# Cross entropy of 256 x 32000 logits on one core: two rows per partition, fourteen loads of shrinking size, one activation table set, and a store without a transpose

## The chip, the core and the metric

The kernel runs on one core of a Trainium2 chip. A core has a matrix engine (TensorE, in the profile PE), a vector engine (VectorE, DVE), an engine for functions such as exp and log (ScalarE, ACT), a general one (GpSimd, POOL), and SyncE (SP), which here only issues transfers. Transfers between the chip's memory and the core's own memory (SBUF, 128 partitions) are moved by 16 DMA engines, whichever engine issued them. Each engine works through its own list in order and waits on semaphores. The metric is the device time of one execution in microseconds, the median of several runs.

## What is computed

The inputs are 256 rows of 32000 float32 logits and one label per row. The result is, for each row, the negative log probability of the label:

```python
log_probs = logits - np.max(logits, axis=-1, keepdims=True)
log_probs = log_probs - np.log(np.sum(np.exp(log_probs), axis=-1, keepdims=True))
return np.array([-log_probs[i, labels[i]] for i in range(batch)]).astype(np.float32)
```

Both kernels leave out the maximum and compute log(sum(exp(x)) * exp(-g)), where g is the row's logit at its label. The logits are 32.77 MB, and each is read once.

## The kernel before

A tile holds one row of logits per partition, so there are two groups of rows, r = 0 (rows 0 to 127) and r = 1 (rows 128 to 255). The columns are cut into eight chunks: six of 4400, one of 3201, one of 2399. The loop goes over the chunks, and in each over the two groups; a step loads 128 x chunk (L120, issued by SP) and takes the exponential in place, with the sum over the row as a second output (L125, on ACT). In the trace such an exponential is two instructions: ACTIVATE, and ACTIVATION_READ_ACCUMULATOR, which writes the sum. Seven buffers of 4400 columns let SP run ahead of ACT; a load into a buffer that was used before waits for the exponential that read it.

Beside this, per group: the labels are loaded by GpSimd's queue (L75, 128 pieces of 8 B, since a label is 64 bits), GpSimd adds the row's offset (L78, L84) and issues an indirect transfer (L87) that gathers g, one float per partition; ACT makes eg = exp(-g) (L94). After the seventh chunk DVE adds up the seven partial sums (L135) and multiplies by eg (L138); this is the bias. When the last sum s_last is there, ACT makes log(s_last * eg + bias) (L143). The order on ACT at the end is chosen by the scheduler of the framework: last exponential of the first group, its logarithm, last exponential of the second group, its logarithm. Exponential and logarithm are taken from two different activation tables, and the compiler puts an ACT_TABLE_LOAD where the function changes.

At the very end the two columns of results (128 partitions x 2) are transposed on TensorE (L152) with an identity matrix made at the start by GpSimd, copied out of its result memory by DVE (L154), and stored by SP as two pieces of 512 B (L157).

Loads share eight semaphores in turn (DMAHW0 to DMAHW7 in the listings below). A load whose semaphore is still in use by an earlier transfer waits until that one has landed.

Of the kernel before, what the change touches and what calls it, by code (L numbers as in the profile page):

```python
# [3 lines left out]

# [5 lines left out]

P = 128

_PLAN = os.environ.get("CE_CHUNKS", "")


def _chunk_plan(C):
    if _PLAN:
        sizes = [int(x) for x in _PLAN.split(",")]
        assert sum(sizes) == C, (sizes, sum(sizes), C)
        return sizes  # L20
    sizes = []
    rem = C
    while rem > 4400 * 2:
        sizes.append(4400)
        rem -= 4400
    if rem > 0:
        a = (rem * 4 + 7) // 7
        a = min(a, rem)
        b = rem - a
        sizes.append(a)  # L30
        if b > 0:
            sizes.append(b)
    assert sum(sizes) == C
    return sizes


@with_exitstack
def kernel(
    ctx: ExitStack,
    tc: tile.TileContext,  # L40
    logits: bass.AP,
    labels: bass.AP,
    out: bass.AP,
):
    nc = tc.nc

    B, C = logits.shape
    n_row_tiles = (B + P - 1) // P
    assert B % P == 0, "only multiples of 128 supported for now"

    sizes = _chunk_plan(C)
    n_chunks = len(sizes)
    F_MAX = max(sizes)

    n_bufs = min(12, max(3, (128 * 1024) // (F_MAX * 4)))
    chunks = ctx.enter_context(tc.tile_pool(name="chunks", bufs=n_bufs))
    small = ctx.enter_context(tc.tile_pool(name="small", bufs=2 * n_row_tiles))
    out_pool = ctx.enter_context(tc.tile_pool(name="outp", bufs=1))

    singles = ctx.enter_context(tc.tile_pool(name="singles", bufs=1))  # L60
    psum_pool = ctx.enter_context(tc.tile_pool(name="psum", bufs=1, space=bass.MemoryType.PSUM))
    id_tile = singles.tile([P, P], mybir.dt.float32)
    make_identity(nc, id_tile[:, :])

    gathered = []
    lbl_t32 = dataclasses.replace(
        labels.tensor,
        shape=[labels.tensor.shape[0] * 2],
        dtype=mybir.dt.int32,
    )  # L70
    for r in range(n_row_tiles):
        r0 = r * P
        lbl = small.tile([P, 2], mybir.dt.int32)
        lbl_dram = bass.AP(tensor=lbl_t32, offset=r0 * 2, ap=[[2, P], [1, 2]])
        nc.gpsimd.dma_start(out=lbl[:, :], in_=lbl_dram)  # L75

        idx = small.tile([P, 1], mybir.dt.int32)
        nc.gpsimd.iota(  # L78
            out=idx[:, :],
            pattern=[[0, 1]],  # L80
            base=r0 * C,
            channel_multiplier=C,
        )
        nc.gpsimd.tensor_add(out=idx[:, :], in0=idx[:, :], in1=lbl[:, 0:1])  # L84

        g = small.tile([P, 1], mybir.dt.float32)
        nc.gpsimd.indirect_dma_start(  # L87
            out=g[:, :],
            out_offset=None,
            in_=logits[:, :],  # L90
            in_offset=bass.IndirectOffsetOnAxis(ap=idx[:, 0:1], axis=1),
        )
        eg = small.tile([P, 1], mybir.dt.float32)
        nc.scalar.activation(  # L94
            out=eg[:, :], in_=g[:, :], func=mybir.ActivationFunctionType.Exp,
            scale=-1.0,
        )
        gathered.append(eg)

    n_bulk = n_chunks - 1  # L100
    partials = [
        small.tile([P, max(1, n_bulk)], mybir.dt.float32, name=f"partial{r}")
        for r in range(n_row_tiles)
    ]
    s_last = [
        small.tile([P, 1], mybir.dt.float32, name=f"s_last{r}")
        for r in range(n_row_tiles)
    ]
    bias_r = [
        small.tile([P, 1], mybir.dt.float32, name=f"bias{r}")  # L110
        for r in range(n_row_tiles)
    ]
    res_all = out_pool.tile([P, n_row_tiles], mybir.dt.float32)

    c0 = 0
    for c, fc in enumerate(sizes):
        for r in range(n_row_tiles):
            r0 = r * P
            x = chunks.tile([P, F_MAX], mybir.dt.float32)
            nc.sync.dma_start(out=x[:, :fc], in_=logits[r0:r0 + P, c0:c0 + fc])  # L120
            if c < n_bulk:
                acc = partials[r][:, c:c + 1]
            else:
                acc = s_last[r][:, :]
            nc.scalar.activation(  # L125
                out=x[:, :fc],
                in_=x[:, :fc],
                func=mybir.ActivationFunctionType.Exp,
                accum_out=acc,
            )  # L130
        c0 += fc
        if c == n_bulk - 1:
            for r in range(n_row_tiles):
                ps = small.tile([P, 1], mybir.dt.float32, name=f"psum{r}")
                nc.vector.reduce_sum(  # L135
                    out=ps[:, :], in_=partials[r][:, :], axis=mybir.AxisListType.X
                )
                nc.vector.tensor_mul(  # L138
                    out=bias_r[r][:, :], in0=ps[:, :], in1=gathered[r][:, :]
                )  # L140

    for r in range(n_row_tiles):
        nc.scalar.activation(  # L143
            out=res_all[:, r:r + 1],
            in_=s_last[r][:, :],
            func=mybir.ActivationFunctionType.Ln,
            scale=gathered[r][:, :],
            bias=bias_r[r][:, :],
        )

    res_t_psum = psum_pool.tile([n_row_tiles, P], mybir.dt.float32, space=bass.MemoryType.PSUM)
    nc.tensor.transpose(out=res_t_psum[:, :], in_=res_all[:, :], identity=id_tile[:, :])  # L152
    res_t = out_pool.tile([n_row_tiles, P], mybir.dt.float32)
    nc.vector.tensor_copy(out=res_t[:, :], in_=res_t_psum[:, :])  # L154

    out_view = out.rearrange("(r p) -> r p", p=P)
    nc.sync.dma_start(out=out_view, in_=res_t[:, :])  # L157


# [1 line left out]
_INS = ['logits', 'labels']  # L161
_OUTS = [((256,), 'float32')]


# [23 lines left out]
```

## Time and profile before

| what | value |
|---|---|
| time, median of 3 runs | 91.57 us (91.46 to 91.59) |
| span of the profiled execution, first to last instruction | 89.6 us |
| median less that span | 1.97 us |
| ACT busy | 63.9 us, 71% of the span |
| POOL busy | 4.5 us |
| DVE and PE busy | 0.9 us and 0.4 us |
| memory read | 32.77 MB, mean 366 GB/s over the span |

The profile gives no time of the profiled execution other than its span; what lies around the span is taken as the difference to the median. A row of the timeline or the chain has start and duration in us, then the engine, the line (L120 is line 120 of the kernel), the operation and "output <- input". SPq stands for SP's list of DMA issues. "[6.86 <-DMA x]" means that the engine stood idle for 6.86 us before and that a load of x ended it. In the rows of groups the numbers are total busy us and mean ns of one. In the rows of windows come the stretch, the busy time of each engine, the clock of TensorE, the DMA share and GB/s.

### The profile page before, as it was taken

How to read it: one execution, taken by the hardware profiler on the slowest of the kernel's cores; microseconds unless marked ns; L12 is line 12 of the kernel's file. 1: busy time of each engine (PE TensorE's matmuls, PEld its weight loads, DVE VectorE, ACT ScalarE, POOL GpSimd, SP SyncE). 2: the span in 40 equal slices, each digit the busy share in tenths (PEclk: the TensorE clock that was granted, in tenths of full speed). 3: DMA queues.
4: the chain of work that ended last, by engine and by line, in shares of the span. 5: the costliest groups of instructions: out<-in, count | busy, mean ns of one | idle time of the engine just before them, and what ended most of it. 6: DMA issues, size and time to landing. Idle time of an engine off the chain costs nothing.

```text
span 89.6 us, 147 instructions
## 1 busy us (share of the span) xinstructions
PE 0.4 (0%) x1; PEld 0.1 (0%) x1; DVE 0.9 (1%) x5; ACT 63.9 (71%) x40; POOL 4.5 (5%) x14
## 2 busy tenths in 40 slices
PE   0000000000000000000000000000000000000010
PEld 0000000000000000000000000000000000000000
DVE  0000000000000000000000000000000010100010
ACT  5000970199999894949769494976949978999950
POOL 5300630000000000000000000000000000000000
DMA  5799999999999999999999999999999999920000
GB/s 118 306 433 393 432 424 417 440 432 416 440 416 448 416 456 416 424 432 424 448 409 424 448 424 440 424 440 416 424 424 423 417 419 428 433 103 0 0 0 0
DMA packets 2436, 32.77 MB, mean 366 GB/s; under 512 B 386, under 2 KB 388, under 8 KB 388
## 3 DMA queue, kind: packets, MB, share of 16 engines
q1 hardware_dynamic: 2308, 32.77, 86.5%
q0 software_dynamic: 128, 0.00, 0.1%
HBM read 32.77 MB, written 0.00 MB: 366 GB/s over the span
## 4 chain that ended last, share of the span: by engine, by line
DMA 74%; ACT 15%; issue 3%; SPq 3%; ACTq 0%; PE 0%; DVE 0%
DMA x<-in_logits_dram 74%; ACT x L125 10%; SPq L120 3%; ACT L143 3%; ACT L125 1%; ACTq L183 0%; PE res_t_psum L152 0%; DVE res_t L154 0%; ACT res_all L143 0%; ACTq L125 0%
## 5 line engine op out<-in xcount | busy, mean ns | idle before, releaser
L125 ACT ACTIVATE x<-x 128x4400 f32<-128x4400 f32 (+2 forms) x16 | 56.5, 3533 | 17.1 <-DMA x<-in_logits_dram 17.0
L94 ACT ACTIVATE eg<-g 128x1 f32<-128x1 f32 x2 | 0.4, 202 | 4.7 <-DMA g<-in_logits_dram,idx 4.7
L125 ACT ACT_TABLE_LOAD x2 | 2.6, 1283 | 0.8 <-PEq L172 0.7
L125 ACT ACTIVATION_READ_ACCUMULATOR x<-x 128x1 f32 x16 | 3.0, 187 | 0.0
L143 ACT ACT_TABLE_LOAD x2 | 2.6, 1283 | 0.0
L87 POOL DMA_INDIRECT g<-in_logits_dram,idx x2 | 2.0, 999 | 0.8 <-DMA lbl<-in_labels_dram 0.5
L75 POOL DMA_DIRECT2D lbl<-in_labels_dram x2 | 1.3, 655 | 0.4 <-issue 0.4
L135 DVE TENSOR_REDUCE psum<-partial 128x1 f32<-128x7 f32 x2 | 0.3, 160 | 76.9 <-ACT x L125 76.9
L143 ACT ACTIVATE res_all<-s_last,bias,eg 128x1 f32<-128x1 f32 x2 | 0.8, 386 | 0.0
L152 PE MATMUL res_t_psum<-id_tile,res_all 128*2 128x128 f32 x1 | 0.4, 371 | 86.6 <-ACT res_all L143 86.6
L84 POOL TENSOR_TENSOR idx<-idx,lbl 128x1 int32<-128x1 int32 x2 | 0.4, 192 | 5.8 <-DMA lbl<-in_labels_dram 5.8
L154 DVE COPY res_t<-res_t_psum 2x128 f32<-2x128 f32 x1 | 0.3, 279 | 9.4 <-PE res_t_psum L152 9.4
masks.py:199 POOL TENSOR_SCALAR_AFFINE_SELECT id_tile<-id_tile 128x128 f32<-128x128 f32 x1 | 0.3, 320 | 0.1
L138 DVE TENSOR_TENSOR bias<-psum,eg 128x1 f32<-128x1 f32 x2 | 0.3, 159 | 0.1
L78 POOL IOTA idx<- 128x1 int32 x2 | 0.3, 140 | 0.0
masks.py:197 POOL MEMSET id_tile<- 128x128 f32 x1 | 0.2, 205 | 0.3 <-POOLq L172 0.3
L152 PEld LDWEIGHTS res_t_psum<-id_tile,res_all 128*2 128x2 f32 x1 | 0.1, 80 | 86.5 <-issue 86.5
L172 POOL MEMSET const-uint8-127<- 128x1 uint8 x1 | 0.1, 119 | 0.0
L172 POOL MEMSET const-bfloat16-1.0<- 128x1 bf16 x1 | 0.1, 113 | 0.0
L172 POOL MEMSET const-float32-0.0<- 128x1 f32 x1 | 0.1, 99 | 0.2 <-issue 0.2
L172 POOL MEMSET const-float32-1.0<- 128x1 f32 x1 | 0.1, 105 | 0.0
## 6 DMA issues: line engine op xcount, KB each, us to landing
x<-in_logits_dram SPq DMA_DIRECT2D x12, 2200.0 KB, 30.9
x<-in_logits_dram SPq DMA_DIRECT2D x2, 1600.5 KB, 30.6
x<-in_logits_dram SPq DMA_DIRECT2D x2, 1199.5 KB, 26.2
lbl<-in_labels_dram POOLq DMA_DIRECT2D x2, 1.0 KB, 7.1
g<-in_logits_dram,idx POOLq DMA_INDIRECT x2, 6.7
out_dram<-res_t SPq DMA_DIRECT2D x1, 1.0 KB
```

Source lines behind the costliest of these rows:

```text
L75: nc.gpsimd.dma_start(out=lbl[:, :], in_=lbl_dram)
L78: nc.gpsimd.iota(out=idx[:, :], pattern=[[0, 1]], base=r0 * C, channel_multiplier=C,)
L84: nc.gpsimd.tensor_add(out=idx[:, :], in0=idx[:, :], in1=lbl[:, 0:1])
L87: nc.gpsimd.indirect_dma_start(out=g[:, :], out_offset=None, in_=logits[:, :], in_offset=bass.IndirectOffsetOnAxis(ap=idx[:, 0:1], axis=1),)
L94: nc.scalar.activation(out=eg[:, :], in_=g[:, :], func=mybir.ActivationFunctionType.Exp, scale=-1.0,)
L120: nc.sync.dma_start(out=x[:, :fc], in_=logits[r0:r0 + P, c0:c0 + fc])
L125: nc.scalar.activation(out=x[:, :fc], in_=x[:, :fc], func=mybir.ActivationFunctionType.Exp, accum_out=acc,)
L135: nc.vector.reduce_sum(out=ps[:, :], in_=partials[r][:, :], axis=mybir.AxisListType.X)
L138: nc.vector.tensor_mul(out=bias_r[r][:, :], in0=ps[:, :], in1=gathered[r][:, :])
L143: nc.scalar.activation(out=res_all[:, r:r + 1], in_=s_last[r][:, :], func=mybir.ActivationFunctionType.Ln, scale=gathered[r][:, :], bias=b ...
L152: nc.tensor.transpose(out=res_t_psum[:, :], in_=res_all[:, :], identity=id_tile[:, :])
L172: nc = _bacc.Bacc("TRN2", target_bir_lowering=False, num_devices=1)
```

## The change

The body of the kernel is written anew, in an order fixed by hand. Partition p now holds rows 2p and 2p+1, one behind the other: 64000 columns, 256000 contiguous bytes. They are cut into fourteen loads that shrink from 14848 to 896 columns; the third crosses from the first row to the second, at column 32000, and gets two exponentials. The first five loads have buffers of their own. The sixth goes into the second's buffer, and the seventh to fourteenth lie one behind the other in the first's.

Labels come in one load of 128 x 16 B, issued by ACT's queue instead of two by GpSimd's. The gathers stay with GpSimd. One instruction makes eg for both rows. A table set with exp and log is loaded ahead of everything. The first row's logarithm is taken in the middle, after the fifth load's exponential; the second's at the end. The results are stored from their 128 partitions, 8 B each, by SP; the identity, the transpose and its copy are gone. (The output's order is the same: partition p's two values are outputs 2p and 2p+1.)

```diff
+CHUNKS = [
+    14848, 12288, 8832, 6528, 4992, 3776, 2752,
+    2368, 1856, 1344, 1344, 1152, 1024, 896,
+]
+HEAD = 5
...
+    flat = logits.rearrange("(p r) c -> p (r c)", r=ROWS)
...
+    for i in range(HEAD):
+        tiles.append((head.tile([P, CHUNKS[i]], F32, name=f"x{i}", tag=f"slot{i}"), starts[i]))
+    mid = head.tile([P, CHUNKS[1]], F32, name="x_mid", tag="slot1")
+    tail = head.tile([P, CHUNKS[0]], F32, name="x_tail", tag="slot0")
...
+    nc.scalar.preload_act_table_set("natural_log_exp_and_others")
...
-    for r in range(n_row_tiles):
-        r0 = r * P
-        lbl = small.tile([P, 2], mybir.dt.int32)
-        lbl_dram = bass.AP(tensor=lbl_t32, offset=r0 * 2, ap=[[2, P], [1, 2]])
-        nc.gpsimd.dma_start(out=lbl[:, :], in_=lbl_dram)
...
+    with tc.manual_schedule():
+        for i in range(HEAD):
+            load(i)
+
+        nc.scalar.dma_start(
+            out=lbl[:, :], in_=bass.AP(tensor=lbl_words, offset=0, ap=[[2 * ROWS, P], [1, 2 * ROWS]])
+        )
+        nc.gpsimd.iota(out=idx[:, :], pattern=[[C, ROWS]], base=0, channel_multiplier=ROWS * C)
+        nc.gpsimd.tensor_add(out=idx[:, :], in0=idx[:, :], in1=lbl[:, 0:2 * ROWS:2])
+        for r in range(ROWS):
+            nc.gpsimd.indirect_dma_start(
...
+        exps(0)
+        for i in range(HEAD + 1, len(CHUNKS)):
+            if i == HEAD + 1:
+                exps(1)
+                load(HEAD)
+            load(i)
+        nc.scalar.activation(out=eg[:, :], in_=g[:, :], func=AF.Exp, scale=-1.0)
+        for i in range(2, len(CHUNKS) - 1):
+            exps(i)
+            if seen[0] == n_of[0] and i == HEAD - 1:
+                nc.vector.reduce_sum(out=sums[:, 0:1], in_=parts[0][:, :], axis=mybir.AxisListType.X)
+                nc.scalar.activation(
+                    out=res[:, 0:1], in_=sums[:, 0:1], func=AF.Ln, scale=eg[:, 0:1]
                 )
...
+        nc.vector.reduce_sum(out=sums[:, 1:2], in_=parts[1][:, :], axis=mybir.AxisListType.X)
+        nc.vector.tensor_mul(out=bias[:, :], in0=sums[:, 1:2], in1=eg[:, 1:2])
+        exps(len(CHUNKS) - 1)
+        nc.scalar.activation(
+            out=res[:, 1:2], in_=s_last[:, :], func=AF.Ln, scale=eg[:, 1:2], bias=bias[:, :]
         )
-
-    res_t_psum = psum_pool.tile([n_row_tiles, P], mybir.dt.float32, space=bass.MemoryType.PSUM)
-    nc.tensor.transpose(out=res_t_psum[:, :], in_=res_all[:, :], identity=id_tile[:, :])
-    res_t = out_pool.tile([n_row_tiles, P], mybir.dt.float32)
-    nc.vector.tensor_copy(out=res_t[:, :], in_=res_t_psum[:, :])
-
-    out_view = out.rearrange("(r p) -> r p", p=P)
-    nc.sync.dma_start(out=out_view, in_=res_t[:, :])
+        nc.sync.dma_start(out=out.rearrange("(p r) -> p r", r=ROWS), in_=res[:, :])
```

How the lists of two engines change is shown by their rows. A row has the line, the operation, output and input, and in brackets the semaphores that it waits on: DMAHW for loads, DMASW for the gathers, Activation, DVE and Pool for work of those engines. The end of ACT's list before, from the last exponential of 3201 columns on:

```order
L125 ACTIVATE x,partial_94<-x 128x3201 [waits DMAHW5_49,Activation_49]
L125 ACTIVATE x,s_last_95<-x 128x2399 [waits DMAHW6_49,Activation_49]
L143 ACT_TABLE_LOAD [waits DVE_49]
L143 ACTIVATE res_all<-s_last_95,bias_97,eg 128x1 [waits Activation_49]
L125 ACT_TABLE_LOAD
L125 ACTIVATE x,s_last_96<-x 128x2399 [waits DMAHW7_49]
L143 ACT_TABLE_LOAD [waits DVE_49]
L143 ACTIVATE res_all<-s_last_96,bias_98,eg 128x1 [waits Activation_49]
```

Three table loads stand among these rows. The start of ACT's list now, up to the sixth load's exponential (x_61 to x_65 are the first five buffers):

```order
L70 ACT_TABLE_LOAD
L102 DMA lbl<-in_labels_dram 128x4
L91 ACTIVATE x_61,parts_68<-x_61 128x14848 [waits DMAHW0_49]
L91 ACTIVATE x_62,parts_68<-x_62 128x12288 [waits DMAHW2_49]
L121 ACTIVATE eg<-g 128x2 [waits DMASW1_49,DMASW0_49]
L91 ACTIVATE x_63,parts_68<-x_63 128x4864 [waits DMAHW3_49]
L91 ACTIVATE x_63,parts_69<-x_63 128x3968
L91 ACTIVATE x_64,parts_69<-x_64 128x6528 [waits DMAHW4_49]
L91 ACTIVATE x_65,parts_69<-x_65 128x4992 [waits DMAHW5_49]
L126 ACTIVATE res<-sums,eg 128x1 [waits DVE_49]
L91 ACTIVATE x_mid,parts_69<-x_mid 128x3776 [waits DMAHW6_49]
```

The one table load is the first row. The exponential of the gathered values stood before behind the first chunk; now it stands behind the second load's exponential, ahead of all the rest. The end of SP's list now, from the sixth load on:

```order
L79 DMA x_mid<-in_logits_dram 128x3776 [waits Activation_49]
L79 DMA x_tail<-in_logits_dram 128x2752
L79 DMA x_tail<-in_logits_dram 128x2368 [waits DMAHW0_49]
L79 DMA x_tail<-in_logits_dram 128x1856 [waits DMAHW1_49]
L79 DMA x_tail<-in_logits_dram 128x1344 [waits DMAHW2_49]
L79 DMA x_tail<-in_logits_dram 128x1344 [waits DMAHW3_49]
L79 DMA x_tail<-in_logits_dram 128x1152 [waits DMAHW4_49]
L79 DMA x_tail<-in_logits_dram 128x1024 [waits DMAHW5_49]
L79 DMA x_tail<-in_logits_dram 128x896 [waits DMAHW6_49]
L135 DMA out_dram<-res 128x2 [waits DMAHW7_49,Activation_49]
```

The sixth load waits for ACT's second exponential, whose buffer it takes. From the eighth on each waits for an earlier transfer on its semaphore: the second 1344 for the third load, 1152 for the fourth, 1024 for the fifth, 896 for the sixth (3776 columns). Before, the eighth to sixteenth loads waited for ACT in the same way, and the store for DVE's copy.

More of the change, by code (lines that the diff above doesn't have):

```diff
@@ L8 @@
 from concourse._compat import with_exitstack
-from concourse.masks import make_identity
 P = 128
[L13 to L34, printed above, removed]
+ROWS = 2
+F32 = mybir.dt.float32
+I32 = mybir.dt.int32
+AF = mybir.ActivationFunctionType
+CHUNKS = [
[3 more added lines that the diff above has]
+HEAD = 5
 @with_exitstack
@@ L47 @@
     B, C = logits.shape
[L48 to L69, printed above, removed]
-    )
-    for r in range(n_row_tiles):
-        r0 = r * P
-        lbl = small.tile([P, 2], mybir.dt.int32)
-        lbl_dram = bass.AP(tensor=lbl_t32, offset=r0 * 2, ap=[[2, P], [1, 2]])
[L75 to L122, printed above, removed]
-            else:
-                acc = s_last[r][:, :]
+    assert B == P * ROWS and sum(CHUNKS) == ROWS * C
@@ new lines @@
+    flat = logits.rearrange("(p r) c -> p (r c)", r=ROWS)
+    pieces = []
+    starts = []
+    at = 0
+    for n in CHUNKS:
+        starts.append(at)
+        cuts = [at] + [c for c in range(C, ROWS * C, C) if at < c < at + n] + [at + n]
+        pieces.append([(a, b, a // C) for a, b in zip(cuts, cuts[1:])])
+        at += n
+    head = ctx.enter_context(tc.tile_pool(name="head", bufs=1))
+    small = ctx.enter_context(tc.tile_pool(name="small", bufs=1))
+    tiles = []
+    for i in range(HEAD):
+        tiles.append((head.tile([P, CHUNKS[i]], F32, name=f"x{i}", tag=f"slot{i}"), starts[i]))
@@ new lines @@
+    mid = head.tile([P, CHUNKS[1]], F32, name="x_mid", tag="slot1")
+    tail = head.tile([P, CHUNKS[0]], F32, name="x_tail", tag="slot0")
+    tiles.append((mid, starts[HEAD]))
+    for i in range(HEAD + 1, len(CHUNKS)):
+        tiles.append((tail, starts[HEAD + 1]))
+    n_of = [sum(1 for ps in pieces[:-1] for q in ps if q[2] == r) for r in range(ROWS)]
+    parts = [small.tile([P, n_of[r]], F32, name=f"parts{r}") for r in range(ROWS)]
+    s_last = small.tile([P, 1], F32, name="s_last")
+    res = small.tile([P, ROWS], F32, name="res")
@@ new lines, with load @@
+    sums = small.tile([P, ROWS], F32, name="sums")
+    bias = small.tile([P, 1], F32, name="bias")
+    lbl = small.tile([P, 2 * ROWS], I32, name="lbl")
+    idx = small.tile([P, ROWS], I32, name="idx")
+    g = small.tile([P, ROWS], F32, name="g")
+    eg = small.tile([P, ROWS], F32, name="eg")
+    nc.scalar.preload_act_table_set("natural_log_exp_and_others")
+    lbl_words = dataclasses.replace(
+        labels.tensor, shape=[labels.tensor.shape[0] * 2], dtype=I32
+    )
+    def load(i):
+        t, base = tiles[i]
+        a, b = starts[i], starts[i] + CHUNKS[i]
+        nc.sync.dma_start(out=t[:, a - base:b - base], in_=flat[:, a:b])
@@ L125, with exps @@
+    seen = [0] * ROWS
+    def exps(i):
+        t, base = tiles[i]
+        for a, b, r in pieces[i]:
+            if i == len(CHUNKS) - 1:
+                acc = s_last[:, :]
+            else:
+                acc = parts[r][:, seen[r]:seen[r] + 1]
+                seen[r] += 1
             nc.scalar.activation(
-                out=x[:, :fc],
-                in_=x[:, :fc],
-                func=mybir.ActivationFunctionType.Exp,
+                out=t[:, a - base:b - base],
+                in_=t[:, a - base:b - base],
+                func=AF.Exp,
@@ L129 @@
                 accum_out=acc,
             )
[L131 to L136, printed above, removed]
-                )
[L138 to L142, printed above, removed]
+    with tc.manual_schedule():
[8 more added lines that the diff above has]
+            nc.gpsimd.indirect_dma_start(
+                out=g[:, r:r + 1],
+                out_offset=None,
+                in_=logits[:, :],
+                in_offset=bass.IndirectOffsetOnAxis(ap=idx[:, r:r + 1], axis=1),
+            )
+        exps(0)
+        for i in range(HEAD + 1, len(CHUNKS)):
+            if i == HEAD + 1:
[9 more added lines that the diff above has]
+                    out=res[:, 0:1], in_=sums[:, 0:1], func=AF.Ln, scale=eg[:, 0:1]
+                )
+        nc.vector.reduce_sum(out=sums[:, 1:2], in_=parts[1][:, :], axis=mybir.AxisListType.X)
+        nc.vector.tensor_mul(out=bias[:, :], in0=sums[:, 1:2], in1=eg[:, 1:2])
+        exps(len(CHUNKS) - 1)
@@ L143 @@
         nc.scalar.activation(
[L144 to L148, printed above, removed]
-        )
-    res_t_psum = psum_pool.tile([n_row_tiles, P], mybir.dt.float32, space=bass.MemoryType.PSUM)
-    nc.tensor.transpose(out=res_t_psum[:, :], in_=res_all[:, :], identity=id_tile[:, :])
-    res_t = out_pool.tile([n_row_tiles, P], mybir.dt.float32)
-    nc.vector.tensor_copy(out=res_t[:, :], in_=res_t_psum[:, :])
```

1 line of the change is left out of this document (removed).

## The prediction

> **What bounds the kernel now.** I read the page first: the busy shares over the span, engine by engine.
>
> ```profile
> span 89.6 us, 147 instructions
> ACT  5000970199999894949769494976949978999950
> DMA  5799999999999999999999999999999999920000
> GB/s 118 306 433 393 432 424 417 440 432 416 440 416 448 416 456 416 424 432 424 448 409 424 448 424 440 424 440 416 424 424 423 417 419 428 433 103 0 0 0 0
> ```
>
> Each of the 40 slices is 2.24 us. The DMA engines are full from the third slice to the 35th; after that they move nothing for four and a half slices, some 10 us, while ACT still works. So there are two stages: a stream of 32.77 MB, and a tail behind it. The windows say the same more finely.
>
> ```profile
> 20.00:66.00 46.00, 0.00 (x0) 0.00 (x0) 0.00 (x0) 37.23 (x20) 0.00 (x0) 1.00 1.00 430
> 79.00:79.50 0.50, 0.00 (x0) 0.00 (x0) 0.00 (x0) 0.48 (x3) 0.00 (x0) 1.00 0.10 38
> 79.50:80.00 0.50, 0.00 (x0) 0.00 (x0) 0.00 (x0) 0.50 (x1) 0.00 (x0) 1.00 0.00 0
> ```
>
> Within 20 to 66 us the DMA share is 1.00 at 430 GB/s (last columns) and ACT is busy 37.23 of 46 us: the loads bound this stage. One column of x is 128 x 4 = 512 B, so 430 GB/s is 1.191 ns a column. No byte moves after 79.5 us.
>
> ACT's timeline gives the landings where an exponential waited for its load, and its own pace where it did not.
>
> ```profile
> 8.88 3.87 ACT L125 ACTIVATE x<-x 128x4400 f32<-128x4400 f32 x1 [6.86 <-DMA x<-in_logits_dram]
> ...
> 66.54 3.87 ACT L125 ACTIVATE x<-x 128x4400 f32<-128x4400 f32 x1 [1.26 <-DMA x<-in_logits_dram]
> ...
> 70.41 2.86 ACT L125 ACTIVATE x<-x 128x3201 f32<-128x3201 f32 x1
> ...
> 74.23 2.87 ACT L125 ACTIVATE x<-x 128x3201 f32<-128x3201 f32 x1 [0.87 <-DMA x<-in_logits_dram]
> ```
>
> The first load was there at 8.88, the twelfth at 66.54: 57.66 us for eleven loads of 4400 columns, 5.24 us each, again 1.191 ns a column. The two loads of 3201 took 74.23 - 66.54 = 7.69, 3.845 each. Two loads of 2399 follow: 2 x 2399 x 1.191 = 5.7, so the last landed at about 79.9. That agrees with the window above.
>
> The tail is the end of the chain of waits (start, us, what).
>
> ```profile
> 79.43 1.28 ACT L143
> 80.71 0.01 issue
> 80.72 0.02 ACT res_all L143
> 80.75 0.38 issue
> 81.13 1.28 ACT L125
> 82.41 0.01 issue
> 82.42 2.30 ACT x L125 x2
> 84.72 0.02 issue
> 84.74 1.28 ACT L143
> 86.02 0.41 ACTq L183
> 86.43 0.14 issue
> 86.56 0.39 PE res_t_psum L152
> 86.95 0.02 issue
> 86.97 0.28 DVE res_t L154
> ```
>
> The three pieces of 1.28 are activation table loads: exp's table is thrown out for the first logarithm, fetched back for the last exponential, and thrown out again. From the last landing at 79.9 to the end at 89.6 are 9.7 us: 2.5 waiting for the first row's logarithm and two table loads, 2.30 for the last exponential, 1.30 for the third table load and its gap, 0.41 for a logarithm, 0.83 for transpose and copy with their gaps (86.43 to 87.25), and, from the row below, 89.6 - 87.28 = 2.32 from the store's issue to the end of the span, plus gaps.
>
> ```profile
> 87.28 0.33 SPq L157 DMA_DIRECT2D out_dram<-res_t  x1
> ```
>
> **The change, part by part.** The sum is made against the span of 89.6. The median of the runs is 91.57; I add the difference, 1.97, unchanged.
>
> *The stream.* All 32.77 MB still go through the same queue. What one transfer costs beyond its bytes comes from two sizes above: 5.24 for 4400 and 3.845 for 3201 give 1.165 ns a column and 0.115 us a transfer. Fourteen transfers instead of sixteen save 0.23 at most and nothing at least; I take 0.15, a last landing at 79.75. The six shortest transfers (1856 columns and under, 0.95 to 0.46 MB) lie below any size in the trace; down to the 1.2 MB loads at its end the 0.115 covers what is seen. The Trainium skill's page "DMA: Bandwidth & Descriptors", section Bandwidth, says the opposite of small loads: to make each at least 1 MiB for 75% of peak, with 341 GB/s at 1 MB. These six are 7616 columns, 3.90 MB: 11.4 us at 341 GB/s against 9.1 by the row, which would put the sum 2.4 us higher. The page's figures are for single transfers and this queue always has several in line; I keep the rows.
>
> *Does the queue stay fed?* In the new order SP's sixth load waits for the second exponential, and from the eighth on each load waits until the load before it on its semaphore has landed. The last (896 columns) waits for the 3776-column load, due near 64.6; its own bytes are due at 78.7, so nothing runs dry. Queued behind that wait is only the store. Five long loads cover the queue to 60 us while the sixth becomes free to issue near 46.5.
>
> *ACT against the landings.* Its costs, by shape:
>
> ```profile
> L125 ACT ACTIVATE x<-x 128x4400 f32<-128x4400 f32 x12 | 46.4, 3866 | 16.2 <-DMA x<-in_logits_dram 16.2
> L125 ACT ACTIVATE x<-x 128x2399 f32<-128x2399 f32 x2 | 4.4, 2202 | 0.0
> ...
> L143 ACT ACTIVATE res_all<-s_last,bias,eg 128x1 f32<-128x1 f32 x2 | 0.8, 386 | 0.0
> ```
>
> (3866 - 2202) / 2001 is 0.832 ns a column. Back to back, the next one starts 70.41 - 66.54 = 3.87 later at 4400: 0.20 + 0.832 n. Alone, from start to sum read, 2399 took 2.30: 0.30 + 0.832 n. With landings counted back from 79.75 at 1.191 ns a column, the first is at 21.2, then 35.8, 46.4, 54.1, 60.1, 64.6, 67.9, 70.7, 72.9, 74.5, 76.1, 77.5, 78.7, 79.75. ACT is late by 0.15 for the third and fourth, 0.3 for the sixth and seventh (where the first row's logarithm, 0.39, stands in its way), 0.15 for the tenth, and free again at each of the last four with 0 to 0.1 to spare. So starting at 21 rather than 9 costs nothing, but ACT has hardly any slack from 46 us on: 1 us lost there is about 0.8 to 1 us at the end. I allow 0.05.
>
> *The tail.* No table load is left in it: the only one stands ahead of everything, in a set that holds both functions. From 79.75: 0.02 to the start, 0.30 + 0.832 x 896 = 1.05, 0.02, the logarithm 0.41, 0.03 to SP, 2.32 from the store's issue to the end: 83.60, with the 0.05 above 83.65. The bias (DVE sum and product) is made while ACT does the last exponential.
>
> *The store.* It goes from 128 partitions in pieces of 8 B instead of two of 512 B; the transpose and its copy (0.83) go. No store of that form is in the trace. The nearest rows are the label loads, 128 pieces of 8 B each:
>
> ```profile
> 1.31 0.71 POOL L75 DMA_DIRECT2D lbl<-in_labels_dram  x1 [0.36 <-issue]
> ...
> 8.82 0.18 POOL L84 TENSOR_TENSOR idx<-idx,lbl 128x1 int32<-128x1 int32 x1 [5.79 <-DMA lbl<-in_labels_dram]
> ...
> 9.57 1.01 POOL L87 DMA_INDIRECT g<-in_logits_dram,idx  x1 [0.49 <-DMA lbl<-in_labels_dram]
> ```
>
> The first landed by 8.82, the second by 9.57: 0.75 apart, on engines full of other work. So 128 pieces cost 0 to 0.75 more than two; I take 0.25, nearer the store's own row, since nothing else is queued. The same page of the Trainium skill, section Specifications, wants at least 512 B a piece, with a read-modify-write below it; that speaks against this store and would put the term at its upper end, the sum 0.5 higher. No row here shows such a write.
>
> The sum is 83.65 + 0.25 = 83.9, and 83.9 + 1.97 = **85.9 us**: 5.7 less. By part: 2.5 for the wait, 1.25 for the shorter last exponential, 1.3 for the last table load, 0.83 for transpose and copy, 0.15 for the stream, less 0.3 for store and backlog.
>
> **What could go otherwise.** *The gathered logits come late (slower, if late enough).* The exponential of the gathered value, eg, now stands on ACT behind the second large exponential and before the third, so everything after 46.5 is queued behind it. Labels and gathers share the DMA engines with the rows of x.
>
> ```profile
> lbl<-in_labels_dram POOLq DMA_DIRECT2D x2, 1.0 KB, 7.1
> g<-in_logits_dram,idx POOLq DMA_INDIRECT x2, 6.7
> ```
>
> The last column is from issue to landing. A row of 17,600 B takes 17,600 / (430/16) = 0.655 us on one of the 16 engines, so 7.1 and 6.7 us are 10.8 and 10.2 rows. If the wait counts in rows, then with first rows of 59,392 B (2.21 us) labels issued at 2.1, behind the one table load, land at 26. POOL needs 0.2 for the index and 1.0 for each gather, to 28.2; 4.2 rows of the second load (49,152 B, 1.83) to 35.8 and 6.0 of the third (1.31) bring the gathered values to 43.7. That is 3 us before eg is due at 46.5. If the wait counts in microseconds, the slack is 28. But the labels now go out on ACT's queue, which moves nothing in this trace. If their pieces take turns with single rows and need twice as many of them, they land near 42 and the gathered values near 55: 8.2 us later than ACT can bear (46.8), 94.1 us. So the point from which it costs is eg's input at 46.8, and at 52.5 the gain is gone. Late but still faster (86.1 to 91.4): chance 0.10; slower: 0.03.
>
> *Long rows or short transfers run slower.* For: no row of 59 KB, no row distance of 256,000 B and no load under 1.2 MB is in the trace. Against: three sizes agree within 1%. Each 1% of rate is 0.76 us; a quarter off the rate in the six shortest alone is 9.1 / 0.75 - 9.1 = 3.0 us, 88.9. The gain is gone at 7.5% over the whole stream, 398 GB/s. The Trainium skill's rule on small loads (above) is a case of this kind. Chance 0.05, of which 0.01 slower.
>
> *Long rows run faster.* If the 0.115 us of a transfer belongs to the 128 rows' starts and long rows save it, or the 448 GB/s slices are real, the stream could reach 436 GB/s, 1.1 us less: 84.8. Chance 0.04.
>
> *The set is loaded again anyway.* The order has one table load, so two more on the path (2.6 us, 88.5) need something it does not show; I give it none of its own.
>
> **How the numbers follow.** The forecast holds with 0.78: 85.9, and by the store's 0 to 0.75, the stream's 0 to 0.23 and a few tenths of backlog 85.5 to 86.7. The range takes in the faster rows below, 84.8, and above the milder delays, to 87.7; left out are gathers later than about 48.5 and a rate down by over 2%, some 0.12 together. The three runs lie within 0.13 us, so about 0.2% can be told from no change. Faster: 0.78 + 0.10 + 0.04 + 0.04 less 0.01 near the line, 0.95; same 0.01; slower 0.04.
>
> **What would show it.** The new profile should have: DMA at 9 until about 79 us and 430 GB/s in 25 to 75 us; one table load; the first exponential at about 21.2; eg not waiting, between the second and third; the last exponential starting within 0.2 of the last landing at 79.75; the store issued near 81.3 and the span ending 2.3 to 3.1 later. A wait on g before eg, an exponential in the tail that starts late with no wait on DMA, a rate under 425 GB/s, or more than 3.1 us behind the store would prove the matching step wrong.

## The result and the profile after

| what | before | after |
|---|---|---|
| time, median | 91.58 us (91.46 to 91.78) | 87.27 us (87.09 to 87.35) |
| after / before | | 0.953 (95%: 0.951 to 0.954) |
| span of the profiled execution | 89.6 us | 85.5 us (its own time 87.28) |
| last exponential starts | 82.42 | 80.23 |
| store issued | 87.28 | 81.72 |
| store's issue to the end of the span | 2.3 us | 3.8 us |

The change gains 4.3 us. The forecast was 5.7 us (85.9), and the result lies inside its range. The head of the new page:

```profile
span 85.5 us, 110 instructions
ACT  6000000000999998199999999999999998999920
DMA  9299999998899998979989998999999999999000
```

A slice is now 2.14 us. But for the second slice the DMA engines are full to the 37th; three slices are left without loads where it was four and a half. (The low second slice is no measure: in a window from 1.5 to 2.0 us the share reads 4.41, more than there can be, so the first long rows are not booked evenly in time.) The timeline of that tail:

```profile
79.14 1.06 ACT L91 ACTIVATE x_tail<-x_tail 128x1024 f32<-128x1024 f32 x1
80.10 0.19 ACT L91 ACTIVATION_READ_ACCUMULATOR x_tail<-x_tail 128x1 f32 x1
80.23 0.95 ACT L91 ACTIVATE x_tail<-x_tail 128x896 f32<-128x896 f32 x1
...
81.08 0.19 ACT L91 ACTIVATION_READ_ACCUMULATOR x_tail<-x_tail 128x1 f32 x1
81.30 0.39 ACT L132 ACTIVATE res<-s_last,bias,eg 128x1 f32<-128x1 f32 x1
81.72 0.35 SPq L135 DMA_DIRECT2D out_dram<-res  x1
```

There is no table load in it. From the last exponential to the store's issue everything is within 0.02 us of the forecast: 1.04 to the sum, 0.41 for the logarithm with its gap, 0.03 to SP. Two things are not: the last exponential starts at 80.23 instead of 79.77, and 85.5 - 81.72 = 3.78 us follow the store's issue, where 2.57 were forecast. The list of issues (KB, us from issue to landing) shows the second one:

```profile
g<-in_logits_dram,idx POOLq DMA_INDIRECT x2, 9.2
lbl<-in_labels_dram ACTq DMA_DIRECT2D x1, 2.0 KB, 20.7
out_dram<-res SPq DMA_DIRECT2D x1, 1.0 KB, 2.9
```

One KB takes 2.9 us to land with nothing else under way. Of the stages before the tail these rows are used further below: the first exponential, eg behind the second one, the exponential of the fifth load, and that of the sixth (x_mid).

```profile
21.31 12.58 ACT L91 ACTIVATE x<-x 128x14848 f32<-128x14848 f32 x1 [19.30 <-DMA x<-in_logits_dram]
...
46.34 0.19 ACT L91 ACTIVATION_READ_ACCUMULATOR x<-x 128x1 f32 x1
46.43 0.19 ACT L121 ACTIVATE eg<-g 128x2 f32<-128x2 f32 x1
...
60.16 4.36 ACT L91 ACTIVATE x<-x 128x4992 f32<-128x4992 f32 x1 [0.19 <-DMA x<-in_logits_dram]
...
64.71 3.33 ACT L91 ACTIVATE x_mid<-x_mid 128x3776 f32<-128x3776 f32 x1
```

So the theory to test is: **the direct store is dear because its 128 pieces of 8 B are written to one spot of memory; it costs more than the transpose and the copy that it replaced, and nearly all of the gain is the table set's.** Rivals: any store takes that long behind this stream; it is the reading from 128 partitions that costs; the gain comes from the shrinking loads.

### The profile page after: what moved, and what is told of

Same layout as the page of the kernel before. It is cut to its first block, busy times and chain, and to the rows that moved or that the text cites. A ratio compares the mean times of both kernels' runs of the same rounds, so it can differ in the third digit from the quotient of the medians.

```text
span 85.5 us, 110 instructions
## 1 busy us (share of the span) xinstructions
DVE 0.5 (1%) x3; ACT 59.0 (69%) x34; POOL 2.6 (3%) x8
## 2 busy tenths in 40 slices
DMA packets 2368, 32.77 MB, mean 383 GB/s; under 512 B 576, under 2 KB 576, under 8 KB 1344
## 4 chain that ended last, share of the span: by engine, by line
DMA 73%; issue 13%; ACT 6%; SPq 3%
DMA x<-in_logits_dram 41%; DMA x_tail<-in_logits_dram 32%; ACT x_tail L91 5%; SPq L79 3%; ACT res L132 0%; ACT x L91 0%; ACT eg L121 0%
## 5 line engine op out<-in xcount | busy, mean ns | idle before, releaser
L91 ACT ACTIVATE x<-x 128x14848 f32<-128x14848 f32 (+5 forms) x6 | 40.7, 6790 | 21.5 <-DMA x<-in_logits_dram 21.5
L91 ACT ACTIVATE x_tail<-x_tail 128x1344 f32<-128x1344 f32 (+6 forms) x8 | 12.2, 1525 | 0.5 <-DMA x_tail<-in_logits_dram 0.4
L91 ACT ACTIVATE x_mid<-x_mid 128x3776 f32<-128x3776 f32 x1 | 3.3, 3332 | 0.0
L91 ACT ACTIVATION_READ_ACCUMULATOR x_tail<-x_tail 128x1 f32 x8 | 1.5, 186 | 0.0
L91 ACT ACTIVATION_READ_ACCUMULATOR x<-x 128x1 f32 x6 | 1.1, 186 | 0.0
```

Of the source, the lines that this page charges most:

```text
L91: nc.scalar.activation(out=t[:, a - base:b - base], in_=t[:, a - base:b - base], func=AF.Exp, accum_out=acc,)
```

## The experiments

A time given without a range is that of a single execution; the four executions of the changed kernel lie within 0.26 us.

### The table set alone

```diff
+    nc.scalar.preload_act_table_set("natural_log_exp_and_others")
     id_tile = singles.tile([P, P], mybir.dt.float32)
```

This is the one line put into the kernel before.

> The kernel before with one part of the change alone: the table set that holds exp and log is loaded at the start. Theory (the table loads held most of the gain: the last exponential waited 2.5 us for them after its data was there, and 1.3 more stood before the last logarithm): the last exponential starts at 79.9, ends at 82.2, logarithm 82.6, transpose, copy and store as before: span 85.8, time about 87.8, nearly all of the change's gain. Rival (the shrinking loads and the two rows per partition hold at least half of it): no more than 2.2 us are gained here, time 89.4 or more.

Measured: 87.45 us, 0.955 of before (0.950 to 0.960), span 85.7. Its tail:

```profile
79.28 0.39 ACT L144 ACTIVATE res_all<-s_last,bias,eg 128x1 f32<-128x1 f32 x1
79.76 2.20 ACT L126 ACTIVATE x<-x 128x2399 f32<-128x2399 f32 x1
...
82.09 0.39 ACT L144 ACTIVATE res_all<-s_last,bias,eg 128x1 f32<-128x1 f32 x1
...
83.33 0.33 SPq L158 DMA_DIRECT2D out_dram<-res_t  x1
```

One line gives 4.1 us; the whole change gives 4.3, and the intervals overlap. The rival is out. The rest of the change nets 0.2 us by the spans, and the two timelines say of what: a shorter last exponential saves 1.25, transpose and copy save 0.8 (82.48 to 83.33 here), the store costs 1.4 (3.78 against 85.7 - 83.33 = 2.37), and the last exponential can start only 0.47 later (80.23 against 79.76).

### The results as one row, one piece of 1 KB

The two columns are turned into a row on TensorE and copied by DVE, as before the change, but side by side in the output's order:

```diff
...
+        for r in range(ROWS):
+            nc.tensor.matmul(row_ps[:, r::ROWS], lhsT=res[:, r:r + 1], rhs=ident[:, :], start=True, stop=True)
+        nc.vector.tensor_copy(out=row[:, :], in_=row_ps[:, :])
-        nc.sync.dma_start(out=out.rearrange("(p r) -> p r", r=ROWS), in_=res[:, :])
+        nc.sync.dma_start(out=out.rearrange("(o n) -> o n", o=1), in_=row[:, :])
```

> The changed kernel, but the results are first turned into one row of 256 values (matmuls with an identity, then a copy by DVE) and stored as one piece of 1 KB. Theory (the 128 pieces of 8 B are what the forecast mis-sized: 3.78 us from the store's issue to the end of the span, where before's two pieces took 2.32): the logarithm ends at 81.7 as now, transpose and copy add about 0.9, and 2.32 follow: span 84.9 to 85.1, time about 86.8, 0.5 us less than the changed kernel though it does more work. Rival (any store takes that long here, because it comes right behind the stream of loads or because of its semaphore): 81.7 + 0.9 + 3.78 = 86.4, time about 88.2.

Measured: 86.56 us (86.52 to 86.58), span 84.8.

```profile
81.71 0.58 PE L143 MATMUL row_ps<-ident,res 128*1 128x128 f32 x2 [16.22 <-ACT res L139]
82.33 0.41 DVE L144 COPY row<-row_ps 1x256 f32<-1x256 f32 x1 [1.69 <-PE row_ps L143]
82.77 0.32 SPq L145 DMA_DIRECT2D out_dram<-row  x1
```

The store is issued 1.05 us later than in the changed kernel, and the program ends 0.7 us earlier: 2.03 from issue to end instead of 3.78. A store behind the same stream need not be slow.

### 128 pieces and 16 pieces from one partition

The row is copied with gaps, so that the store is cut into pieces of 8 B or of 64 B:

```diff
-    row = small.tile([1, ROWS * P], F32, name="row")
+    row = small.tile([1, 128, 4], F32, name="row")
...
-        nc.vector.tensor_copy(out=row[:, :], in_=row_ps[:, :])
-        nc.sync.dma_start(out=out.rearrange("(o n) -> o n", o=1), in_=row[:, :])
+        nc.vector.tensor_copy(out=row[:, :, 0:2], in_=row_ps[:, :].rearrange("o (k w) -> o k w", w=2))
+        nc.sync.dma_start(out=out.rearrange("(o k w) -> o k w", o=1, w=2), in_=row[:, :, 0:2])
```

These lines are against the kernel with one piece. The second kernel has a tile of 1 x 16 x 18, and 16 for 2.

> As the run with one piece, but the row lies in SBUF with gaps, so that the store is 128 pieces of 8 B again, all from one partition. Theory (the number of small pieces written to memory costs): from the store's issue to the end 3.5 to 3.9 us, as with 128 partitions, span about 86.4. Rival (it is the 128 partitions that are read, not the pieces): 2.3 to 2.5, span about 85.0.

> As the run with one piece, but the row lies in SBUF with gaps, so that the store is 16 pieces of 64 B, one for each DMA engine. If the cost grows with the number of pieces on one engine (8 there, 1 here): 2.3 to 2.6 us from the store's issue to the end. If any piece much shorter than 512 B pays the full price: 3.5 to 3.9.

128 pieces: 89.12 us, span 87.3. The issue, and its time to landing in the list of issues:

```profile
82.77 0.59 SPq L145 DMA_DIRECT2D out_dram<-row  x1
```

```profile
out_dram<-row SPq DMA_DIRECT2D x1, 1.0 KB, 3.7
```

16 pieces: 87.24 us, span 85.5, and in its list of issues:

```profile
82.85 0.59 SPq L145 DMA_DIRECT2D out_dram<-row  x1
```

```profile
out_dram<-row SPq DMA_DIRECT2D x1, 1.0 KB, 1.7
```

From the issue to the end 128 pieces take 4.5 us and 16 take 2.65. Both lie above what was expected; 0.27 of it is the issue, which takes 0.59 instead of 0.32 for pieces that lie in one partition. Of the two readings for 16 pieces it is the first that holds, nearly. The order is clear: 128 from one partition cost as much as 128 from 128 partitions and more; pieces of 64 B, short as they are, cost little. Reading from many partitions is not it. The differences are well above what varies between runs: over the changed kernel and the four runs below that store 128 neighbouring pieces of 8 B, issue to end is 3.7 to 4.1 us; over the three that store one piece, 2.0 to 2.1.

### The pieces spread in memory, and the control

The last store goes to scratch memory, once 4096 B apart and once side by side (2 for 1024):

```diff
+    scratch = nc.dram_tensor("scratch", (P, 1024), F32, kind="Internal").ap()
...
+        nc.sync.dma_start(out=out.rearrange("(p r) -> p r", r=ROWS), in_=eg[:, :])
...
-        nc.sync.dma_start(out=out.rearrange("(p r) -> p r", r=ROWS), in_=res[:, :])
+        nc.sync.dma_start(out=scratch[:, 0:ROWS], in_=res[:, :])
```

> The changed kernel, but the last store writes its 128 pieces of 8 B into scratch memory, 4096 B apart; the output proper gets only eg, early, so the result is left out. If small pieces cost because all 128 fall into the same 1 KB of memory (writes to one place wait for each other): 1.1 to 1.6 us to landing, 2.1 to 2.6 from the store's issue to the end, span about 84.2. If each small piece costs wherever it goes: 2.9 to landing and 3.8 to the end as now, span about 85.5.

> The control for the spaced store: the last store again goes into scratch memory, but its 128 pieces of 8 B lie side by side in 1 KB there; the output proper gets only eg, early, so the result is left out. Theory (pieces that fall into the same 1 KB wait for each other): 3.6 to 4.1 us from the store's issue to the end as in the changed kernel, where the spaced pieces took 2.6. Rival (scratch memory, or the earlier store of eg, made the spaced store fast): 2.6 again.

Spread, in the timeline and in the list of issues (86.19 us, span 84.4):

```profile
81.82 0.33 SPq L138 DMA_DIRECT2D scratch<-res  x1
```

```profile
scratch<-res SPq DMA_DIRECT2D x1, 1.0 KB, 1.5
```

Side by side (87.19 us, span 85.4):

```profile
81.67 0.33 SPq L138 DMA_DIRECT2D scratch<-res  x1
```

```profile
scratch<-res SPq DMA_DIRECT2D x1, 1.0 KB, 2.7
```

The instruction is the same, and so are the pieces; 1.2 us hang on where they fall (2.6 from issue to end against 3.7). So most of the price is neither the number of pieces nor their size alone but that such small pieces are all written into one KB. One KB alone does not do it either: the 16 pieces of 64 B fill the same stretch and landed in 1.7. The trace records sixteen completions of each of these two stores, and they show where the time goes. Spread, they come from 1.23 to 1.52 us after the issue; side by side the first comes at 1.23 too, but the last at 2.67. That looks like writes waiting for each other; what makes them wait, and from which distance on they no longer do, was not tried. The spread pieces still take 0.55 more than the one piece of 1 KB; that much may be their number.

### Two table sets again

```diff
-    nc.scalar.preload_act_table_set("natural_log_exp_and_others")
```

> The changed kernel without its common table set: exp and log are in two sets again, so a load of 1.28 us stands before the first row's logarithm, one behind it, and one before the last. Theory (ACT has almost no slack against the landings from 46 us on): the two in the middle put ACT 2.6 us back at 67, of which 1.6 are left at the last exponential; with the last load 2.9 more in all, span 88.4, time about 90.2. Rival (the loads of x bound the stream, ACT catches up): 1.3 more, 88.6.

Measured: 90.29 us, span 88.5.

```profile
64.53 1.28 ACT L125 ACT_TABLE_LOAD   x1
65.82 0.29 ACT L125 ACTIVATE res<-sums,eg 128x1 f32<-128x1 f32 x1
66.13 1.28 ACT L90 ACT_TABLE_LOAD   x1
67.43 3.35 ACT L90 ACTIVATE x_mid<-x_mid 128x3776 f32<-128x3776 f32 x1
...
81.94 0.93 ACT L90 ACTIVATE x_tail<-x_tail 128x896 f32<-128x896 f32 x1
...
82.98 1.28 ACT L131 ACT_TABLE_LOAD   x1
```

ACT falls 2.7 us back in the middle and is still 1.7 us late at the last exponential; the last table load adds its 1.3. In this plan of loads ACT is nearly as tight as the DMA engines, as the forecast worked out, and the common set is worth 3.0 us in it.

### A long last load, and twelve loads

```diff
-    2368, 1856, 1344, 1344, 1152, 1024, 896,
+    2368, 1856, 1344, 1344, 3072,
```

> The changed kernel with its last three loads (1152, 1024, 896 columns) as one of 3072, twelve loads in all. Theory (each transfer costs some 0.07 us, and the last exponential 0.832 ns a column): last landing 0.14 earlier, at 80.05, the last exponential 0.30 + 2.56 = 2.86 instead of 1.05: 1.7 us more, 88.9. Rival (short loads are dear, as the rule on 1 MiB has it): the last landing is earlier by 0.4 or more, at 79.8 or before, and the time below 88.7.

Measured: 89.28 us, span 87.5.

```profile
80.05 2.76 ACT L91 ACTIVATE x_tail<-x_tail 128x3072 f32<-128x3072 f32 x1 [2.26 <-DMA x_tail<-in_logits_dram]
...
83.36 0.35 SPq L135 DMA_DIRECT2D out_dram<-res  x1
```

The last exponential, which waits for its load, starts 0.18 us earlier with two loads fewer, 0.09 a load; the exponential costs what it should. Short loads are cheap, and the shrinking end is worth 1.64 us up to the store's issue (83.36 against 81.72). (From there this kernel took 4.1 rather than 3.8, which the expectation did not have.)

### A better tail

With eg on the diagonal of a matrix, one matmul scales the sum and turns it into a row; the logarithm is taken of the row, and there is no copy:

```diff
...
+            nc.vector.tensor_scalar_mul(out=dg[r][:, :], in0=ident[:, :], scalar1=eg[:, r:r + 1])
...
+        nc.tensor.matmul(ps1[:, :], lhsT=sums[:, 1:2], rhs=dg[1][:, :], start=True, stop=False)
...
+        nc.tensor.matmul(ps1[:, :], lhsT=s_last[:, :], rhs=dg[1][:, :], start=False, stop=True)
+        nc.scalar.activation(out=row[:, 1::ROWS], in_=ps1[:, :], func=AF.Ln)
+        nc.sync.dma_start(out=out.rearrange("(o n) -> o n", o=1), in_=row[:, :])
```

> The changed kernel with another tail: a matmul with eg on the diagonal scales and turns the sums into a row in one step (the bias is summed into it), ACT takes the logarithm of that row, and the row is stored as one piece of 1 KB. There is neither a copy by DVE nor a store of small pieces. By the theory (small pieces cost, and each step behind the last exponential is paid in full): the last exponential ends at 81.3, matmul to 81.75, logarithm to 82.1, 2.03 from the store's issue to the end as in the run with one piece: span 84.1 to 84.3, time 85.9 to 86.1. If short steps between engines cost more than their parts show, 86.5 as with the copy.

Measured: 86.05 us (85.90 to 86.14), 0.940 of before (0.939 to 0.942), span 84.3.

```profile
81.36 0.58 PE L140 MATMUL ps<-dg,s_last 128*1 128x128 f32 x2 [0.18 <-ACT x_tail L97]
81.98 0.27 ACT L141 ACTIVATE row<-ps 1x128 f32<-1x128 f32 x1 [0.67 <-PE ps L140]
82.28 0.32 SPq L142 DMA_DIRECT2D out_dram<-row  x1
```

It beats the changed kernel by 1.2 us, by the terms that were expected. A plan of twelve loads was tried on top of it (4672, 3520, 2624, 2048, 1536, 1152, 960 after the first five):

> The run that takes the logarithm of the row, with twelve loads instead of fourteen: after the first five come 4672, 3520, 2624, 2048, 1536, 1152, 960 columns, each as long as ACT can bear. Theory (each transfer costs some 0.07 to 0.08 us, ACT's time follows 0.20 + 0.832 n): last landing 0.15 earlier, last exponential 0.05 longer: 0.1 us less, 85.95, hardly to be told from 86.05. Rival (ACT runs late with the longer steps): 86.2 to 86.5.

Measured: 86.03 us (85.97 to 86.37): no difference that can be told between these two plans of loads.

### The labels late

```diff
+        exps(0)
+        exps(1)
         nc.scalar.dma_start(
             out=lbl[:, :], in_=bass.AP(tensor=lbl_words, offset=0, ap=[[2 * ROWS, P], [1, 2 * ROWS]])
...
-        exps(0)
         for i in range(HEAD + 1, len(CHUNKS)):
             if i == HEAD + 1:
-                exps(1)
                 load(HEAD)
```

> The changed kernel with the labels issued late: ACT issues their load when its second exponential begins, at 36 us, instead of at 0.8. This tries the forecast's slower rival: what a late eg costs, and what the wait is counted in. If label pieces and gathers take turns with the rows of x: eight turns of 1.31 us and the rows in line ahead, labels at 48 to 52, gathered values at 56 to 60, and the end 9.5 to 13 us later, 97 to 100. If their wait counts in microseconds as in the kernel before: labels at 43.5, gathered values at 53, 93.5. If ACT could catch up: less than half of either.

Measured: 98.59 us, span 96.8.

```profile
35.78 10.44 ACT L91 ACTIVATE x<-x 128x12288 f32<-128x12288 f32 x1 [1.85 <-DMA x<-in_logits_dram]
35.79 0.36 ACTq L104 DMA_DIRECT2D lbl<-in_labels_dram  x1
...
49.35 0.20 POOL L108 TENSOR_TENSOR idx<-idx,lbl 128x2 int32<-128x2 int32 x1 [48.39 <-DMA lbl<-in_labels_dram]
...
58.88 0.20 ACT L121 ACTIVATE eg<-g 128x2 f32<-128x2 f32 x1 [12.56 <-DMA g<-in_logits_dram,idx]
```

```profile
lbl<-in_labels_dram ACTq DMA_DIRECT2D x1, 2.0 KB, 13.4
```

eg starts 12.4 us later than in the changed kernel (46.43 there), and the end is 11.3 us later. So the rival on the slower side was a real one: the forecast charged it a microsecond for each that eg is late, the run 0.91, and only its point of decision was not reached.

## Why the forecast was right, and where its sizes were off

**The table loads.** Right. 2.5 us of wait and 1.3 of the last load were to go; the table set alone gave 4.1 us.

**The last exponential and the logarithm.** Right: 1.51 us from the last exponential's start to the store's issue were forecast, 1.49 came.

**The store.** This is the term that failed: 2.32 + 0.25, with 0.75 as the highest extra; it took 3.78, 1.46 extra, and more than 3.1 was the forecast's own sign of being wrong here. The bound came from the two label loads, 128 pieces of 8 B that landed 0.75 us apart. How far apart two loads land is not the price of their pieces, and those pieces are read from memory and written to 128 partitions. The store writes them to memory, all into one KB, and the spread store with its control shows that this is what costs: about 1.2 us of it. The transpose and copy of 0.83 that the direct store replaced were cheaper than what came instead, as the runs with one piece show (0.7 and 1.2 us less than the changed kernel). The Trainium skill's page "DMA: Bandwidth & Descriptors", section Specifications, had warned of pieces under 512 B, and the sign is as it says. Its 512 B do not give the size here: pieces of 64 B took 2.65 us from issue to end, and 8 B pieces 4096 B apart 2.58, where the two pieces of 512 B before took 2.32. No run shows whether there is a read-modify-write.

**The stream.** The last landing was to come at 79.75, between 0 and 0.23 us before that of the kernel before; it came at about 80.2. (The 79.9 that it had read for the kernel before was right: the last completion is at 79.89. But the window that it called in agreement has no byte after 79.5 and does not show it.)

Short loads cost 0.09 us each (the long last load), close to the 0.115 that the forecast had read from two sizes. The forecast took fewer transfers to mean less time, and the saving on the long ones did not appear: the second to fifth load, 32640 columns, took from 21.31 to 60.16, 1.190 ns a column, where the loads of 4400 before took 1.191 with all that a transfer costs. The nine short ones, 16512 columns, took from there to 80.2, 1.21 ns a column.

Over 25 to 75 us the DMA engines moved 423 GB/s (429 before), just under the 425 that the forecast named as a sign of being wrong. The sixteen completions of the last load lie between 79.30 and 80.20; before, between 79.32 and 79.89. So the first comes when it came before, and the last, for which ACT waits, comes later; the first load's already lie 0.95 us apart, between 20.34 and 21.29. Why they do was not tried.

The rule on 1 MiB in the Trainium skill's page "DMA: Bandwidth & Descriptors", section Bandwidth, is not borne out by loads that stand in line one behind the other. (The page's table is of transfers issued by GpSimd, here SP issues them; that its figures are for single transfers is the forecast's reading.) Two rows of the changed kernel's timeline show it:

```profile
70.86 2.18 ACT L91 ACTIVATE x_tail<-x_tail 128x2368 f32<-128x2368 f32 x1 [0.25 <-DMA x_tail<-in_logits_dram]
...
80.23 0.95 ACT L91 ACTIVATE x_tail<-x_tail 128x896 f32<-128x896 f32 x1
```

The six loads of 0.46 to 0.95 MB came between 70.86 and 80.23: 3.90 MB in 9.37 us, 416 GB/s, where the estimate from the page's 341 GB/s was 11.4 us and that from the row 9.1.

**ACT's slack.** Nearly right: from 46 us on, most of what ACT loses is paid for at the end. The forecast had 0.8 to 1 us at the end for each lost. With the labels late it was 0.91 (11.3 of 12.4); without the common set 0.63 (1.7 of the 2.7 lost in the middle).

**The gathered values.** Right that eg would not wait (46.43, right behind the second exponential); how the wait is counted was right for the labels only. The forecast had the gathered values at 43.7 us if waits count in rows, and 28 us before eg was due if they count in microseconds. The labels went out at 0.77, while the table load still ran, not behind it at 2.1, and landed 20.7 us later at 21.5. The run with late labels landed them in 13.4 us beside shorter rows, and before it was 7.1 beside rows of 17,600 B: for the labels it is rows that count. For the gathers neither count holds: from issue to landing they took 6.7 us before, 8.1 and 10.4 in the changed kernel, whose rows beside them are 2.8 times as long, and 7.2 with the labels late. (The forecast also counted 10.8 rows of 59,392 B up to 26, though by its own landings the last of these rows is in at 21.2.) So the gathered values were there by 34.2, some 12 us before eg was due, where the forecast by rows left 3.

**The sum.** 83.9 was forecast for the span, 85.5 came: 1.21 by the store, 0.45 by the stream, less 0.05 of backlog that did not arise. Around the span lay 1.8 us instead of 1.97. That the result still lies inside the range is luck in part: for its own mechanism the forecast had 85.5 to 86.7, and 87.27 is above that. The range went up to 87.7 to leave room for late gathers and a slower stream, not for a store that takes 1.46 us more.

## What to carry to other kernels

When a function's table is thrown out between the last data and the last result, put that right first; here one line was worth as much as the whole rewrite. A transpose in a tail is not waste if it turns a store of many small pieces into one long piece: price both ways by the time from the store's issue to the end. A row that reads small pieces from memory says nothing on writing them there.

## What the runs showed of the hardware

- 128 pieces of 8 B written side by side into 1 KB of memory took 2.7 to 3.1 us from issue to landing (3.7 where they lay in one partition); the same pieces 4096 B apart took 1.5, and 16 pieces of 64 B took 1.7.
- A small load that shared the DMA engines with long rows waited by rows: 2 KB of labels, in pieces of 16 B, took 20.7 us beside rows of 59,392 B, and 13.4 us when most of the rows beside them had 35,328 B.
- ACT's queue issues a transfer while ACT itself is busy: the labels went out at 35.79, as the exponential of 10.4 us began.
- Six loads of 0.46 to 0.95 MB in line one behind the other ran at 416 GB/s; two short loads fewer made 0.18 us.
